# A two-layer decoder trunk on one core: projections and NSA scores as single plain float32 matmuls on unsplit operands

## The chip, the core and the metric

The kernel runs on one core of a Trainium2 chip. The core has TensorE (matmuls, written PE in the profile, its weight loads PEld), VectorE (DVE), ScalarE (ACT), GpSimd (POOL) and SyncE (SP), which here issues all transfers between HBM and the on-chip memory. The metric is the device time of one execution in microseconds, as the median of several runs.

## What is computed

Two layers, each on 256 tokens of width 1024: a modulation of the condition vector, a normalised and modulated input h, one projection to 3864 columns, two attention groups on them (MoBA, which here is plain causal attention, and NSA with a compressed, a selected and a window branch), a gated concatenation y, an output projection, a norm and a gated residual. Cut to what matters here:

```python
def reference(x, c, w_ada, ..., w_in, w_out, ...):
    cs = jax.nn.silu(c)
    for l in range(DEPTH):                        # 2
        mod = cs @ w_ada[l] + b_ada[l]
        shift, scale, gate = ...
        h = rmsnorm(x, g_pre[l]) * (1.0 + scale) + shift
        u = h @ w_in[l]                           # 256 x 1024 @ 1024 x 3864
        (qm, km, vm, zm, qn, kc, vc, ks, vs, kw, vw, gl, zn) = split(u)
        # per head: softmax(q k^T - slope * distance) v; NSA: three branches, gated by sigmoid(gl)
        y = concat([o_m * silu(zm), o_n * silu(zn)])
        y = y @ w_out[l]                          # 256 x 1024 @ 1024 x 1024
        x = x + gate * rmsnorm(y, g_post[l])
    return x
```

All inputs and the output are float32.

## The kernel before

Every projection is a sum over 8 row blocks of 128. Its operands are split into a high part, rounded to float32r, and a low part, the rest: `split_hi` and `split_lo` (lines 360 to 374) make `hi` and `lo` of each weight unit of 128 x 1024 on ScalarE or VectorE, and h and y are kept as `hH`, `hL` and `yH`, `yL`. `mm3` (lines 396 to 401) then makes one product from three float32r matmuls: low by high, high by low, high by high. Most have 256 moving columns; the token projection of the first stage (line 839) has 512, the combined one of layer 1 and the rest of the values 280. The scores of NSA's two full branches (lines 586, 587) are two float32r matmuls, of a query tile that holds the high part on one half of the partitions and the low part on the other (`qs`), with the keys' low and high parts (`kL`, `kH`). MoBA's scores (615, 617), all products of probabilities and values (596 to 630), the modulation (216) and the matmuls that only keep the array busy (283) are plain float32. Transposes (565 and others) are matmuls with the identity in a mode of their own.

The first layer's start (`first_layer_start`, from line 774) is in the order in which it is written: five stages of 1, 1, 2, 2 and 2 row blocks, each with the next stage's modulation between its column blocks. All that follows is put in order by the framework's scheduler from the steps in `PLAN`, so that projections of one step fill TensorE between the attention steps of another. A letter d in a step sends the high parts to VectorE. Weights come in units of up to 512 KB through the pool `raw` (8 buffers), and go from there to the pool `split` (8 buffers each of `hi` and `lo`). SyncE issues their loads in order, each as soon as its buffer is free. `out_mm` is the output projection of one token tile, `post` the norm and residual behind it, `hnorm` the next layer's h. `tables` writes the distance biases (`bias`, `cbias`) before the first attention.

## Time and profile before

| | us |
|---|---|
| median of 3 runs | 356.67 (354.29 to 356.84) |
| profiled execution, first to last instruction | 354.4 |
| PE busy | 341.4 |
| DVE busy | 266.1 |
| ACT busy | 204.3 |
| mean DMA rate | 201 GB/s |

The profiled execution's time is known as its span, 354.4 us; the runs without a profile lie between 0.1 us below and 2.4 us above it. A busy time sums the lengths of instructions. A matmul's length in the profile is its way through the array, some 280 ns for most, while the next one starts earlier; what a matmul costs in a stream is the distance from its start to the next start. A plain float32 matmul that is no transpose stands in the trace as two MATMUL records, each with a weight load: line 283 has 20 matmuls in the program and 40 records.

### The profile page before, as it was taken

To read this page: it belongs to the slowest core of one execution; us is meant where nothing else is said; L and a number is where in the kernel's file an instruction comes from. 1 tells how busy PE (TensorE), PEld (TensorE's weight loads), DVE (VectorE), ACT (ScalarE), POOL (GpSimd) and SP (SyncE) were. 2 spreads that over 40 slices of the span, in tenths; PEclk is the share of its full clock that TensorE was granted. 3 is DMA by queue.
4 is the path that set the end of the run, shared out by engine and by line. 5 is a ranking of instruction groups with operands and counts; after the bars stand their busy time and mean duration, and the time that the engine had idled before them with its cause. 6 is when DMAs were issued, how large, how long until landed. Compare 5 with 4: busy or idle time off the path is not lost.

```text
span 354.4 us, 7595 instructions
## 1 busy us (share of the span) xinstructions
PE 341.4 (96%) x2852; PEld 299.6 (85%) x2852; DVE 266.1 (75%) x727; ACT 204.3 (58%) x506; POOL 10.5 (3%) x23
## 2 busy tenths in 40 slices
PE   7999999999999999989999999999999999999993
PEld 7789889988887878767998999998878898677993
DVE  2648669999987898879898985999987646776132
ACT  4423407776989863757365455543889655668211
POOL 2000001100000000000011000000000000000000
PEclk9999999999999999999999999999999999999998
DMA  7999999939955566899755798489454330000111
GB/s 237 321 331 353 350 338 220 308 108 354 347 186 154 167 217 210 259 351 333 197 149 162 223 284 247 130 285 352 130 160 139 119 120 2 0 2 1 62 60 59
DMA packets 72060, 71.12 MB, mean 201 GB/s; under 512 B 11440, under 2 KB 61784, under 8 KB 72024
## 3 DMA queue, kind: packets, MB, share of 16 engines
q1 hardware_dynamic: 72024, 70.65, 64.1%
q8 instruction: 22, 0.36, 0.4%
q14 instruction: 14, 0.11, 0.1%
HBM read 69.58 MB, written 1.06 MB: 199 GB/s over the span
## 4 chain that ended last, share of the span: by engine, by line
PE 73%; DVE 13%; DMA 6%; issue 4%; ACT 2%; POOL 1%; SPq 1%; DVEq 0%; POOLq 0%; ACTq 0%
PE pj L399 13%; PE pj L400 13%; PE pj L401 13%; PE tr L565 5%; DVE lo L372 4%; PE av L602 3%; PE tr L216 3%; DMA yL<-in_w_ada_dram 2%; DMA raw<-in_w_out_dram 2%; PE av L627 2%; PE sc L586 2%; PE sc L617 2%; PE av L604 2%; PE pj L839 2%; PE av L596 2%
## 5 line engine op out<-in xcount | busy, mean ns | idle before, releaser
L372 DVE TENSOR_TENSOR lo<-raw,hi 128x1024 fp32r<-128x1024 f32 (+3 forms) x82 | 90.7, 1123 | 15.9 <-ACT hi L364 15.5
L399 PE MATMUL pj<-hH,lo 128*128 128x256 f32 x320 | 93.1, 291 | 0.0
L400 PE MATMUL pj<-hL,hi 128*128 128x256 f32 x320 | 92.5, 289 | 0.0
L401 PE MATMUL pj<-hH,hi 128*128 128x256 f32 x320 | 92.1, 288 | 0.0
L364 ACT CAST hi<-raw 128x1024 fp32r<-128x1024 f32 (+4 forms) x70 | 66.0, 966 | 22.7 <-PE pj L401 17.1
L399 PEld LDWEIGHTS pj<-hH,lo 128*128 128x128 f32 x320 | 61.0, 191 | 4.4 <-issue 3.4
L400 PEld LDWEIGHTS pj<-hL,hi 128*128 128x128 f32 x320 | 61.0, 191 | 2.2 <-issue 1.7
L401 PEld LDWEIGHTS pj<-hH,hi 128*128 128x128 f32 x320 | 61.0, 191 | 1.4 <-issue 1.1
L548 ACT ACTIVATE S<-S,mn 128x128 f32<-128x128 f32 (+1 forms) x96 | 42.7, 448 | 4.4 <-DVE mn L545 4.1
L233 DVE SCALAR_TENSOR_TENSOR acc<-raw,cs,acc 128x512 f32<-128x512 f32 x49 | 36.5, 747 | 1.6 <-DMA raw<-in_w_ada_dram 1.2
L545 DVE CUSTOM_DVE_ANT_0 S<-sc,bias 128x128 f32<-128x128 f32 (+1 forms) x96 | 31.6, 350 | 7.6 <-PE tr L565 3.1
L399 PE MATMUL pj<-hi,yL 128*128 128x256 f32 x112 | 31.9, 285 | 0.0
L401 PE MATMUL pj<-hi,yH 128*128 128x256 f32 x112 | 31.9, 286 | 0.0
L400 PE MATMUL pj<-lo,yH 128*128 128x256 f32 x112 | 31.8, 285 | 0.0
L565 PE MATMUL tr<-ident,S 128*128 128x128 f32 x144 | 29.6, 281 | 0.0
L570 ACT COPY PT<-tr 128x384 f32<-128x384 f32 x44 | 20.3, 478 | 10.0 <-PE tr L565 9.9
L565 PEld LDWEIGHTS tr<-ident,S 128*128 128x128 f32 x144 | 17.5, 140 | 6.7 <-issue 3.0
L555 ACT ACTIVATE S<-S,sm 128x256 f32<-128x256 f32 (+1 forms) x46 | 20.4, 483 | 2.9 <-DVE sm L550 1.4
L399 PEld LDWEIGHTS pj<-hi,yL 128*128 128x128 f32 x112 | 21.2, 189 | 0.9 <-issue 0.9
L401 PEld LDWEIGHTS pj<-hi,yH 128*128 128x128 f32 x112 | 21.1, 189 | 0.5 <-issue 0.5
L400 PEld LDWEIGHTS pj<-lo,yH 128*128 128x128 f32 x112 | 21.0, 188 | 0.3 <-issue 0.3
L548 ACT ACTIVATION_READ_ACCUMULATOR S<-S,mn 128x1 f32 x96 | 18.3, 190 | 0.0
(248 smaller groups left out, 650.1 us busy)
## 6 DMA issues: line engine op xcount, KB each, us to landing
raw<-in_w_in_dram SPq DMA_DIRECT2D x43, 512.0 KB, 4.5
raw<-in_w_ada_dram SPq DMA_DIRECT2D x32, 512.0 KB, 4.6
raw<-in_w_out_dram SPq DMA_DIRECT2D x16, 512.0 KB, 7.2
raw<-in_w_in_dram SPq DMA_DIRECT2D x9, 256.0 KB, 3.9
qs<-in_w_ada_dram SPq DMA_DIRECT2D x4, 512.0 KB, 7.2
yH<-in_w_ada_dram SPq DMA_DIRECT2D x4, 512.0 KB, 7.2
yL<-in_w_ada_dram SPq DMA_DIRECT2D x4, 512.0 KB
raw<-in_w_in_dram SPq DMA_DIRECT2D x9, 128.0 KB, 5.7
```

Source lines behind the costliest of these rows:

```text
L216: self.nc.tensor.matmul(pm[32 * r:32 * r + 32, :P], self.csz[:, k, :], raw[:, j, c * P:(c + 1) * P], start=first <= k < first + turns, sto ...
L233: nc.vector.scalar_tensor_tensor(out=out, in0=raw[:, j], scalar=self.cs[:, k:k + 1], in1=out, op0=OP.mult, op1=OP.add)
L364: self.nc.scalar.copy(hi[:, :nk * n], raw[:, :nk * n])
L372: self.nc.vector.tensor_sub(lo[:, :nk * n], raw[:, :nk * n], hi[:, :nk * n].bitcast(F32))
L399: nc.tensor.matmul(out, aL, bH, start=first, stop=False)
L400: nc.tensor.matmul(out, aH, bL, start=False, stop=False)
L401: nc.tensor.matmul(out, aH, bH, start=False, stop=last)
L545: nc.vector.tensor_tensor_reduce(out=s[:, a:b], in0=sc[:, a:b], in1=self.bias[:, h, S - (b - a):S], scale=-1.0, scalar=3.0e38, op0=OP.add, ...
L548: nc.scalar.activation(s[:, a:b], s[:, a:b], AF.Exp, bias=mn[:, i:i + 1], scale=-1.0, accum_out=sm[:, i:i + 1])
L555: nc.scalar.activation(s[:, a:b], s[:, a:b], AF.Copy, scale=sm[:, i:i + 1])
L565: nc.tensor.transpose(pt[:, i * P:(i + 1) * P], blk, self.ident)
L570: nc.scalar.copy(ps, pt[:, :3 * P])
```

## The change

h, y, the weights, and NSA's queries and keys are kept once, as float32. Each product that `mm3` made of three float32r matmuls is now one plain float32 matmul; the score of NSA's full branches is one plain float32 matmul on the 64 partitions of the head, with the keys `ks` copied to both halves. All splitting is gone: the casts, the subtractions, the pool `split`, and the tiles of the second parts. The pool `raw` has 24 buffers, from which TensorE now reads the weights directly; the first layer's modulation weights, which had the place of later tiles, come through it too. The output weights come in units of 2 row blocks by 512 columns instead of 4 by 256, so that most of `out_mm` has 512 moving columns. The step letters d, now without meaning, are gone. Comments were removed, so all lines have other numbers. The core of the diff:

```diff
-0post0 1h0 0out1 0post1 1V00:d 1h1 1V10 0na 1A0 1V01:d 1C:d 1V11 1A1 1K:d 1Q0 1Q1 1cmp0
+0post0 1h0 0out1 0post1 1V00 1h1 1V10 0na 1A0 1V01 1C 1V11 1A1 1K 1Q0 1Q1 1cmp0
...
-            nc.scalar.copy(self.hH[:, ks, ts], hT[:, ks])
-            nc.vector.tensor_sub(self.hL[:, ks, ts], hT[:, ks], self.hH[:, ks, ts].bitcast(F32))
...
-        return raw, nk, n
-    def split_hi(self, unit, tags=None, eng=None):
-        raw, nk, n = unit
-        hi = self.tl(self.mp if tags else self.hp, [P, UNIT], tags[0] if tags else "hi", F32R)
-        if eng == 1 or eng is None and "d" not in self.how:
-            self.nc.scalar.copy(hi[:, :nk * n], raw[:, :nk * n])
-        else:
-            self.nc.vector.tensor_copy(hi[:, :nk * n], raw[:, :nk * n])
-        return hi
-    def split_lo(self, unit, hi, tags=None):
-        raw, nk, n = unit
-        lo = self.tl(self.mp if tags else self.hp, [P, UNIT], tags[1] if tags else "lo", F32R)
-        self.nc.vector.tensor_sub(lo[:, :nk * n], raw[:, :nk * n], hi[:, :nk * n].bitcast(F32))
-        return (hi[:, :nk * n].rearrange("p (k c) -> p k c", k=nk),
-                lo[:, :nk * n].rearrange("p (k c) -> p k c", k=nk))
-    def split(self, unit, tags=None):
-        """The two f32r parts of a unit (in slots of self.mp if tags are given)."""
-        return self.split_lo(unit, self.split_hi(unit, tags), tags)
-    def load_split(self, pieces, nk, n, tags=None):
-        return self.split(self.load(pieces, nk, n), tags)
-    def weights(self, w, cols, tags=()):
-        """Both f32r parts of the columns, a list over the 8 row blocks."""
+        return rv
...
-            hv, lv = self.load_split([wv[:, k0:k0 + nk, a:b] for a, b in cols], nk, n,
-                                     tags[k0 // step] if k0 // step < len(tags) else None)
-            parts += [(hv[:, j], lv[:, j]) for j in range(nk)]
+            v = self.load([wv[:, k0:k0 + nk, a:b] for a, b in cols], nk, n)
+            parts += [v[:, j] for j in range(nk)]
...
-    def mm3(self, out, aH, aL, bH, bL, first, last):
-        """out (+)= a.T @ b from f32r parts: low terms first."""
-        nc = self.nc
-        nc.tensor.matmul(out, aL, bH, start=first, stop=False)
-        nc.tensor.matmul(out, aH, bL, start=False, stop=False)
-        nc.tensor.matmul(out, aH, bH, start=False, stop=last)
...
-            hv, lv = parts[k]
-            self.mm3(pj[:, :n], self.hH[:, k, ts], self.hL[:, k, ts], hv, lv, k == 0, k == KK - 1)
+            self.nc.tensor.matmul(pj[:, :n], self.h[:, k, ts], parts[k],
+                                  start=k == 0, stop=k == KK - 1)
...
-                self.mm3(pj[:, b * S + lo:b * S + hi], hv[:, bs], lv[:, bs],
-                         self.hH[:, k, lo:hi], self.hL[:, k, lo:hi], k == 0, k == KK - 1)
+                self.nc.tensor.matmul(pj[:, b * S + lo:b * S + hi], parts[k][:, bs],
+                                      self.h[:, k, lo:hi], start=k == 0, stop=k == KK - 1)
...
-                q = self.qs[j][:, b, qt * P:(qt + 1) * P]
-                nc.tensor.matmul(o, q, self.kL[:, g, :, :nk], start=True, stop=False)
-                nc.tensor.matmul(o, q, self.kH[:, g, :, :nk], start=False, stop=True)
+                rows = slice(j * HD, (j + 1) * HD)
+                nc.tensor.matmul(o, self.qn[rows, b, qt * P:(qt + 1) * P],
+                                 self.ks[rows, g, :, :nk], start=True, stop=True)
...
-        y = self.tl(self.mp, [P, S], "ytmp", bufs=1)
-        nc.vector.scalar_tensor_tensor(out=y, in0=av[:, :S], scalar=0.5,
+        nc.vector.scalar_tensor_tensor(out=self.y[:, blk, :], in0=av[:, :S], scalar=0.5,
                                        in1=self.z[blk // 4][:, blk % 4, :],
                                        op0=OP.mult, op1=OP.mult)
-        nc.scalar.copy(self.yH[:, blk, :], y)
-        nc.vector.tensor_sub(self.yL[:, blk, :], y, self.yH[:, blk, :].bitcast(F32))
...
-        for c in range(4):
-            hv, lv = self.load_split([w[:, k0:k0 + 4, c * 256:c * 256 + 256]], 4, 256)
-            for j in range(4):
-                self.parts[c, k0 + j] = (hv[:, j], lv[:, j])
+        for c in range(2):
+            for k in range(k0, k0 + 4, 2):
+                v = self.load([w[:, k:k + 2, c * 512:c * 512 + 512]], 2, 512)
+                for j in range(2):
+                    self.parts[c, k + j] = v[:, j]
...
-            for c in range(a // 256, b // 256):
-                for k in k4:
-                    hv, lv = self.parts[c, k]
-                    self.mm3(pos[i][:, c * 256 - a:c * 256 - a + 256], self.yH[:, k, ts],
-                             self.yL[:, k, ts], hv, lv, k == 4 and c * 256 == a,
-                             k == 3 and c * 256 + 256 == b)
+            for k in k4:
+                v = self.parts[a // 512, k][:, a % 512:a % 512 + b - a]
+                self.nc.tensor.matmul(pos[i][:, :b - a], self.y[:, k, ts], v,
+                                      start=k == 4, stop=k == 3)
...
-        self.kH = self.tl(self.tp, [P, NG, 2, S], "wide", F32R)
-        self.kL = self.tl(self.tp, [P, NG, 2, S], "wide", F32R)
+        nc = self.nc
+        self.ks = self.tl(self.mp, [P, NG, 2, S], "ks")
         v = pj.rearrange("p (i k) -> p i k", i=2)
         half = [slice(0, HD), slice(HD, P)]
         for g in range(NG):
-            for r in (g, 1 - g):
+            for r in range(2):
                 if r == g:
-                    nc.scalar.copy(self.kH[half[r], g], v[half[g]])
+                    nc.scalar.copy(self.ks[half[r], g], v[half[g]])
                 else:
-                    nc.vector.tensor_copy(self.kH[half[r], g], v[half[g]])
-        for g in range(NG):
-            for r in range(2):
-                nc.vector.tensor_sub(self.kL[half[r], g], v[half[g]],
-                                     self.kH[half[g], g].bitcast(F32))
+                    nc.vector.tensor_copy(self.ks[half[r], g], v[half[g]])
...
-            for n, (h, v) in enumerate(((self.hH, w[0]), (self.hL, w[0]), (self.hH, w[1]))):
-                for t in range(NT):
-                    for j, k in enumerate(ks):
-                        nc.tensor.matmul(pA[t], h[:, k, t * P:(t + 1) * P], v[:, j],
-                                         start=(k == 0 and n == 0), stop=(k == KK - 1 and n == 2))
+            for t in range(NT):
+                for j, k in enumerate(ks):
+                    nc.tensor.matmul(pA[t], self.h[:, k, t * P:(t + 1) * P], w[:, j],
+                                     start=k == 0, stop=k == KK - 1)
...
-                self.mm3(dst[:, (b % 2) * S:(b % 2 + 1) * S], w[0][:, j, bs],
-                         w[1][:, j, bs], self.hH[:, k], self.hL[:, k],
-                         k == 0 and b % 2 == 0, k == KK - 1 and b % 2 == 1)
+                nc.tensor.matmul(dst[:, (b % 2) * S:(b % 2 + 1) * S], w[:, j, bs], self.h[:, k],
+                                 start=k == 0 and b % 2 == 0, stop=k == KK - 1 and b % 2 == 1)
...
-            hT = self.tl(self.wp, [P, n, S], "S")
             for j, k in enumerate(ks):
-                nc.vector.tensor_scalar(hT[:, j], xT[k // 4][:, k % 4], self.mod[:, 8 + k:9 + k],
-                                        self.mod[:, k:k + 1], op0=OP.mult, op1=OP.add)
-            hi = self.split_hi(uw[0], None, HIGH_ENGINE[s])
-            nc.scalar.copy(self.hH[:, kc], hT)
-            nc.vector.tensor_sub(self.hL[:, kc], hT, self.hH[:, kc].bitcast(F32))
-            w = [self.split_lo(uw[0], hi)] + [self.split(u) for u in uw[1:]]
+                nc.vector.tensor_scalar(self.h[:, k], xT[k // 4][:, k % 4],
+                                        self.mod[:, 8 + k:9 + k], self.mod[:, k:k + 1],
+                                        op0=OP.mult, op1=OP.add)
+            w = uw
...
-            self.rp = self.pool("raw", bufs=8)
-            self.hp = self.pool("split", bufs=8)
+            self.rp = self.pool("raw", bufs=24)
```

At the first stage of the start, TensorE's rows before (`av` from line 283 is the matmul that only keeps the array busy; `pj` and `sc` are sums in PSUM, `tr` transposes; the operands stand as moving, stationary):

```order
L283 MATMUL av_213<-ident 128x128 x6
L839 MATMUL pj_220<-hi_228,hH_167 128x512
L839 MATMUL pj_221<-hi_228,hH_167 128x512
L839 MATMUL pj_220<-hi_228,hL_168 128x512
L839 MATMUL pj_221<-hi_228,hL_168 128x512
L839 MATMUL pj_220<-lo_232,hH_167 128x512
L839 MATMUL pj_221<-lo_232,hH_167 128x512
L813 MATMUL tr_267<-ident,z_149 128x128 x4
L813 MATMUL tr_273<-ident,modG_153 128x128 x4
L399 MATMUL pj_222<-hH_167,lo_236 128x256
L400 MATMUL pj_222<-hL_168,hi_234 128x256
L401 MATMUL pj_222<-hH_167,hi_234 128x256
```

and now:

```order
L277 MATMUL av_209<-ident 128x128 x6
L764 MATMUL pj_216<-raw_109,h_164 128x512
L764 MATMUL pj_217<-raw_109,h_164 128x512
L739 MATMUL tr_240<-ident,z_146 128x128 x4
L739 MATMUL tr_246<-ident,qn_150 128x128 x4
L772 MATMUL pj_218<-h_164,raw_113 128x256
```

Six matmuls became two, and three became one, in the same places; the operands come straight from `raw` and `h`.

At the first scores of NSA's full branches in layer 0, TensorE's rows before (`wide` is kL or kH, `qs` the query of both parts):

```order
L586 MATMUL sc_1151<-wide_883,qs_135_909 128x256
L587 MATMUL sc_1151<-wide_882,qs_135_909 128x256
L400 MATMUL pj_1354<-hL_168,hi_1344 128x256
L401 MATMUL pj_1354<-hH_167,hi_1344 128x256
L399 MATMUL pj_1354<-hH_167,lo_1352 128x256
L400 MATMUL pj_1354<-hL_168,hi_1350 128x256
```

and now:

```order
L544 MATMUL sc_764<-ks_595,qn_616 128x256
L544 MATMUL sc_777<-ks_595,qn_616 128x512
L544 MATMUL sc_802<-ks_595,qn_616 128x256
L554 MATMUL av_763<-pct_734,vx_707 64x256 x2
L381 MATMUL pj_945<-h_164,raw_941 128x256 x2
L544 MATMUL sc_815<-ks_595,qn_616 128x512
L523 MATMUL tr_790<-ident,S_766 128x128
L523 MATMUL tr_796<-ident,S_766 128x128
```

A score is one matmul instead of two, and the projections between scores are single matmuls, one or two at a time.

On VectorE at the start of the program, the rows before (`cs` is silu(c), `rstd` the norm's factor):

```order
L137 MEMSET hmask 128x8
L145 MEMSET kbd 128x64
L165 SCALAR_TENSOR_TENSOR cs<-cth,tr_125 128x8
L167 TENSOR_SCALAR cs<-cs 128x8
L168 COPY csz<-cs 128x8
L303 SCALAR_TENSOR_TENSOR rstd_157<-ssq_150 128x1
L322 TENSOR_SCALAR z_149<-x_97,rstd_157 128x512 x2
```

and now:

```order
L134 MEMSET hmask 128x8
L142 MEMSET kbd 128x64
L110 TENSOR_SCALAR bias<-S_547 128x256 x8
L121 TENSOR_SCALAR cbias<-S_561 128x2x16 x8
L162 SCALAR_TENSOR_TENSOR cs<-cth,tr_122 128x8
L164 TENSOR_SCALAR cs<-cs 128x8
L165 COPY csz<-cs 128x8
L297 SCALAR_TENSOR_TENSOR rstd_154<-ssq_147 128x1
```

The tables, which used to follow the last stage's h, now stand ahead of silu(c): the buffer of their distances (`S`) is no longer taken by the unsplit h of the stages. On GpSimd their two distances and their masks moved ahead of the first `rstd` in the same way.

## Rows read from the trace of the kernel before

**Rows 1.** The page, parts 1, 2 and 4: busy time, granted clock, DMA in slices, chain.

```profile
PE 341.4 (96%) x2852; PEld 299.6 (85%) x2852; DVE 266.1 (75%) x727; ACT 204.3 (58%) x506; POOL 10.5 (3%) x23
...
PEclk9999999999999999999999999999999999999998
DMA  7999999939955566899755798489454330000111
...
PE 73%; DVE 13%; DMA 6%; issue 4%; ACT 2%; POOL 1%; SPq 1%; DVEq 0%; POOLq 0%; ACTq 0%
```

**Rows 2.** Busy time in two stretches, microseconds, instructions behind each.

```profile
55.00:75.00 20.00, 19.76 (x198) 18.70 (x196) 19.64 (x42) 14.92 (x29) 2.75 (x3) 1.00 0.74 202
200.00:220.00 20.00, 20.00 (x166) 19.83 (x165) 14.48 (x21) 9.40 (x17) 0.00 (x0) 1.00 0.89 244
```

**Rows 3.** Who TensorE waited for: total, times, longest, in microseconds.

```profile
PE tr L252 <- ACT accr L245: 2.0, 3, 1.2
...
PE tr L336 <- DVE wide L322: 1.2, 2, 0.7
PE pj L400 <- DVE lo L372: 0.9, 1, 0.9
```

**Rows 4.** The page, part 5: groups of instructions, busy time and mean ns.

```profile
L372 DVE TENSOR_TENSOR lo<-raw,hi 128x1024 fp32r<-128x1024 f32 (+3 forms) x82 | 90.7, 1123 | 15.9 <-ACT hi L364 15.5
L399 PE MATMUL pj<-hH,lo 128*128 128x256 f32 x320 | 93.1, 291 | 0.0
...
L364 ACT CAST hi<-raw 128x1024 fp32r<-128x1024 f32 (+4 forms) x70 | 66.0, 966 | 22.7 <-PE pj L401 17.1
```

**Rows 5.** TensorE in order of time: start, length, 59 to 66 us.

```profile
58.97 0.28 PE L399 MATMUL pj<-hH,lo 128*128 128x256 f32 x1
59.08 0.28 PE L400 MATMUL pj<-hL,hi 128*128 128x256 f32 x1
...
66.04 0.28 PE L401 MATMUL tr<-hH,hi 128*128 128x256 f32 x1
```

**Rows 6.** TensorE in order of time at 11.7 us, plain float32, two records a matmul.

```profile
11.74 1.50 PE L283 MATMUL av<-ident 128*128 128x128 f32 x12
```

**Rows 7.** Line 283: durations in ns, minimum, median, maximum.

```profile
L283 PE MATMUL av<-ident x40: 275/276/582, 1.4 to 13.0; 128*128 128x128 f32 x40
```

**Rows 8.** TensorE in order of time at 142 us: a float32 score, then float32r.

```profile
141.81 0.59 PE L617 MATMUL sc<-km,qm 64*128 64x256 f32 x2
142.33 0.39 PE L399 MATMUL pj<-hH,lo 128*128 128x256 f32 x1
142.55 0.28 PE L400 MATMUL pj<-hL,hi 128*128 128x256 f32 x1
```

**Rows 9.** Line 617: durations in ns, minimum, median, maximum.

```profile
L617 PE MATMUL sc<-km,qm x32: 376/377/480, 139.6 to 322.5; 64*128 64x256 f32 x32
```

**Rows 10.** TensorE in order of time at 100 us: transposes, NSA scores, projections.

```profile
100.31 0.27 PE L565 MATMUL tr<-ident,S 128*128 128x128 f32 x1
100.34 0.36 PE L401 MATMUL pj<-hH,hi 128*128 128x256 f32 x1
...
100.89 0.39 PE L587 MATMUL sc<-wide,qs 128*128 128x512 f32 x1
101.12 0.28 PE L399 MATMUL pj<-hH,lo 128*128 128x256 f32 x1
...
101.47 0.28 PE L399 MATMUL pj<-hH,lo 128*128 128x256 f32 x1
101.68 0.44 PE L602 MATMUL av<-PT,vsw 128*64 128x256 f32 x2
```

**Rows 11.** VectorE in order of time at 6 and at 54 to 62 us.

```profile
6.04 0.16 DVE L303 SCALAR_TENSOR_TENSOR rstd<-ssq 128x1 f32<-128x1 f32 x1 [2.57 <-ACT z L309]
...
54.60 0.89 DVE L113 TENSOR_SCALAR bias<-S 128x256 bf16<-128x256 f32 x4
...
60.83 1.71 DVE L124 TENSOR_SCALAR cbias<-S 128x32 f32<-128x32 f32 x8
```

**Rows 12.** GpSimd in order of time, 55 to 65 us.

```profile
60.98 1.10 POOL L114 TENSOR_SCALAR_AFFINE_SELECT bias<-bias 128x1024 bf16<-128x1024 bf16 x1 [18.16 <-DVE bias L113]
62.60 1.65 POOL L126 TENSOR_SCALAR_AFFINE_SELECT cbias<-cbias 128x128 f32<-128x128 f32 x2 [0.53 <-DVE cbias L124]
```

More of the change, by code (lines that the diff above doesn't have):

```diff
@@ L10 @@
 F32 = mybir.dt.float32
-F32R = mybir.dt.float32r
 BF16 = mybir.dt.bfloat16
@@ L784, in loads @@
             k, n = STAGES[s]
-            slots = []
-            while len(slots) < 2 * n:
-                tag, m = tags.pop(0)
-                t = self.tl(self.mp, [P, m, UNIT], tag)
-                slots += [t[:, i] for i in range(m)]
-            ada = self.ada_loads(l, spec[s], slots)
+            ada = self.ada_loads(l, spec[s])
             ks = slice(k, k + n)
```

53 lines of the change are left out of this document (14 added, 39 removed).

## The prediction

> **What bounds the kernel now.** I read the busy times first. TensorE (PE) is busy 341.4 of 354.4 us, VectorE 266.1, ScalarE 204.3; TensorE's granted clock stands at its upper level (2.4 GHz) in every slice but the last, and the chain that ended last is 73% TensorE [rows 1]. Busy TensorE time can hide slack, since lengths overlap, so the next look was at stretches. At 200 to 220 us nothing but TensorE is full. At 55 to 75 us VectorE is just as full (19.64 of 20), so the chain's 13% of VectorE could mean that the splits set the pace there [rows 2]. The order of time says no: from 58.97 to 66.04 us 60 float32r matmuls start at even distances, 7.07 / 59 = 0.120 us, with no hole [rows 5]. And the list of TensorE's waits is short, its three largest after the start being 2.0, 1.2 and 0.9 us in total [rows 3]. TensorE streams nearly all the time, VectorE and ScalarE run beside it. So the time after the change is, in the first place, the old time plus what TensorE gains or loses in issue.
>
> **What one product costs before and after.** Starts are what counts here, not lengths. Before: three float32r matmuls of 256 columns at 0.120 us, 0.360 us [rows 5]; with 512 columns one takes 101.12 - 100.89 = 0.23 us [rows 10]; with 280 about 0.130, on the line between.
>
> After: a plain float32 matmul. None with 128 rows, 128 stationary columns and 256 moving columns is in the trace, but two neighbours are. The array-warming matmul has the full array and 128 moving columns: 12 records last 1.50 us, the last of them 0.276, so a start every (1.50 - 0.276) / 11 = 0.111 us [rows 6, 7]. MoBA's score has 64 rows and 256 columns: two records last 0.59 us, the last 0.376, so 0.59 - 0.376 = 0.214 us between starts [rows 8, 9]. Twice the columns, twice the distance: a record costs about 0.0008 us a column and next to nothing besides, thus 0.216 for 256, 0.236 for 280, 0.431 for 512. The length grows with the columns too, 276 to 376 ns, as that of a float32r matmul does. Every plain float32 matmul is two records, so 0.432, 0.472 and 0.862 us. A float32r matmul goes past 256 columns in 0.120 us, a pair of plain records takes 3.6 times that. Three matmuls for one is no gain at this exchange.
>
> **The sum, part by part.** (a) The projections. The program has 544 products of 256 columns, 32 of 280 and 16 of 512 (320 of the first stand in one row [rows 4], the others in smaller ones). Before: 544 x 0.360 + 32 x 0.390 + 16 x 0.69 = 195.8 + 12.5 + 11.0 = 219.3 us. After, with the output projection in wider pieces: 448 of 256, 32 of 280 and 64 of 512 columns, 448 x 0.432 + 32 x 0.472 + 64 x 0.862 = 193.5 + 15.1 + 55.2 = 263.8 us. **Plus 44.5 us**. All of it lies on TensorE, which has no hole to take it.
>
> (b) The NSA scores, 16 of 256 and 16 of 512 columns: two float32r matmuls each before, 16 x 0.24 + 16 x 0.46 = 11.2 us, one plain one after, 16 x 0.432 + 16 x 0.862 = 20.7 us. **Plus 9.5 us.** They now use 64 rows of the array, and two scores of the two halves could run beside each other where they stand next to each other; the order shows that at few places, so I take nothing off, and 3 us for the low end.
>
> (c) Changes of the array's shape. Between a matmul on the full array and one on part of it TensorE loses some 0.09 us: line 399 to line 602 takes 101.68 - 101.47 = 0.21 instead of 0.12 [rows 10], and line 617 to 399 takes 0.31 (the second record starts at 142.02, the next matmul at 142.33) instead of 0.21; then the second float32r matmul waits another 0.10, 142.55 - 142.33 = 0.22 [rows 8]. The rows of TensorE in their order have 151 such changes before and 184 after, because the scores left the full shape: 33 x 0.09 = +3.0 us. The second wait, 44 times before, should vanish in a record that lasts 0.21 anyhow: 44 x 0.10 = -4.4 us. Transposes end for free against a float32r matmul (100.34 - 100.31 = 0.03 us between starts [rows 10]); bursts of them that run into a projection or score fall from 79 to 54, each worth 0.08: +2.0 us. Together **plus 0.6 us**. What no row shows is whether a plain full-array matmul beside a transpose counts as a change of shape. If not, this stands; if so, 99 places pay 0.09 and the 54 ends cost 0.08 more, +13 us. I take the first, since float32r and transposes, also of different kinds, follow each other on the full array at no cost.
>
> (d) The splits. VectorE loses its 82 subtractions (90.7 us) and more, ScalarE the 70 casts (66.0 us) [rows 4]. This is beside TensorE's work and worth only the waits that it caused: 0.9 us for `lo`, part of the 1.2 before the transposes of layer 1's h [rows 3], and the steps between h's modulation and its first matmul. **Minus 2 us**; the bounds are 0 and 6, the whole of TensorE's waits behind the start. Chains around TensorE get shorter while TensorE gets slower, so I see no new wait on these two engines.
>
> (e) The transfers. The bytes stay, and DMA is near full only in slices up to some 55 us and a few later ones [rows 1]. TensorE now needs longer for each byte, and 24 buffers (up to 8 of them held by output weights) let loads run ahead. Cost 0; the cover is TensorE's own slowness, and without it the old waits for DMA, under 1 us each, would be back.
>
> (f) The tables at the start. On VectorE 2 x 0.89 + 1.71 = 3.5 us now stand ahead of silu(c) and the first `rstd`, where VectorE was idle for 2.57 us before 6.04 us and had 1.5 more before that [rows 11]; on GpSimd 1.10 + 1.65 = 2.75 us stand ahead of the first `rstd` power [rows 12]. If VectorE starts them at 1.5 us it is through at 5.0, GpSimd then at 6.7, and `rstd`, due at 6.2, is 0.5 late. The first modulation matmul waits for weights until 8.37, so 0 to 0.5 us; I take 0. The 3.5 us that VectorE saves at 54 to 62 us are worth nothing, as TensorE streams there.
>
> Sum: 44.5 + 9.5 + 0.6 - 2 = +52.6 us, from 354.4 to 407.0 us of span. The median of the runs is 2.3 us above that span; the forecast goes by it: 356.7 + 52.6 = **409 us**.
>
> **Rivals.** *Weight loads set the pace.* The float32r matmuls start every 0.120 us and each has a weight load; at 200 to 220 us the loads are busy 19.83 of 20 us [rows 2]. If the load, not the columns, made the 0.120, a plain record would take that too, and three loads would become two: 592 products x 0.120 saved is -71 us, also -2 for waits, thus 356.7 - 73 = **284 us**, much faster. It holds if records of 256 columns start less than 0.18 us apart. Against it: 0.214 with 256 columns and 0.111 with 128, each with one load [rows 6 to 9]. The Trainium skill, "Perfetto Trace Analysis", section "Identifying the Most-Contended Engine", says to judge TensorE's headroom by the busy share of its weight loads and not by that of matmuls; by that rule the 85% of PEld would make fewer loads a gain, as in this rival. The trace disagrees for plain float32, where the same one load goes with 0.111 or 0.214 us.
>
> *Transposes pay.* The 13 us of (c): **422 us**. For it: all plain matmuls of the trace that border on transposes, on parts of the array, pay. Against it: they also change the shape.
>
> *The second half's weights are not hidden.* If each of the 576 plain matmuls paid the 0.10 us of the second matmul after a change [rows 8], +58 us: **467 us**. Line 283 speaks against it, whose 40 records load weights each and keep 0.111 [rows 6, 7].
>
> *All waits go, and the scores run in pairs.* 409 - 4 - 3 = **402 us**, from the lower ends of (b) and (d).
>
> **How the numbers follow.** The forecast and the last rival, which is its lower edge, have 0.80; transposes that pay 0.12, hidden weights 0.03, weight loads that set the pace 0.04; 0.01 is left for anything near no change. The range runs from 354.3, the fastest run, + 52.6 - 7 = 400 to the 422 of the transposes, rounded to 399 and 424: it leaves out the third rival and the faster one. Slower by over 1%, which is about what a measurement here can tell from no change: 0.95; within 1%: 0.01; faster: 0.04.
>
> **What would show it.** Plain records of 256 columns 0.21 to 0.22 us apart in the start's last stage, which then takes 20 matmuls x 2 x 0.216 = 8.6 us for its ten column blocks instead of 7.2; TensorE the chain's main part, above 80%; VectorE near 145 us busy, ScalarE near 120; the last slices unchanged. Starts 0.12 apart would refute (a), 0.30 or more between the last record of a projection and a transpose would show (c) wrong, and long waits of TensorE for `raw` transfers would refute (e).

## The result, and the profile after

The changed kernel takes 414.88 us (median of 4 runs, 414.59 to 415.35) where the kernel before takes 356.26 (4 runs): a ratio of 1.166, 95% interval 1.162 to 1.169, so 16.6% slower. Its profiled execution took 414.95 us, with a span of 413.2; the span grew by 58.8 us. The forecast was 409 us in a range of 399 to 424. Direction and range held, and the time is 5.9 us above the forecast.

The page of the kernel after, parts 1, 2 and 4: busy time, granted clock and DMA in slices, chain by engine.

```profile
PE 402.5 (97%) x2164; PEld 280.4 (68%) x2164; DVE 159.2 (39%) x590; ACT 129.1 (31%) x401; POOL 8.2 (2%) x23
...
PEclk9999999999999999999999999999999999999998
DMA  8999999999673059986075369970000000000111
...
PE 94%; DVE 2%; ACT 1%; issue 1%; POOL 0%; POOLq 0%; DVEq 0%; ACTq 0%
```

Against [rows 1]: TensorE makes up 94% of the chain instead of 73%. VectorE is busy 159 us instead of 266 and ScalarE 129 instead of 204, and the kernel is slower: what left these engines had been holding next to nothing up. The granted clock stands at the upper level (2.4 GHz) in every slice but the last, as before, so no part of the loss is a slower clock. DMA all but stops in the last quarter, where TensorE still streams: the weights are there before TensorE wants them.

Who TensorE of the kernel after waited for (total, times, longest, in us); the three largest:

```profile
PE av L277 <- POOL ident masks.py:199: 1.7, 1, 1.7
PE tr L328 <- DVE wide L316: 1.2, 1, 1.2
PE tr L246 <- ACT accr L239: 0.8, 2, 0.4
```

No wait is for a weight transfer. The wait for `lo` [rows 3] is gone, and so is more than half of that for `accr`. What is left to explain lies in TensorE's own records. Its rows in order of time (start, length), in the last stage of the start and at 99 to 104 us:

```profile
64.34 1.89 PE L772 MATMUL pj<-h,raw 128*128 128x256 f32 x8
66.06 3.62 PE L772 MATMUL sc<-h,raw 128*128 128x256 f32 x16
69.52 1.89 PE L772 MATMUL av<-h,raw 128*128 128x256 f32 x8
71.24 1.89 PE L772 MATMUL tr<-h,raw 128*128 128x256 f32 x8
73.06 0.24 PE L395 MATMUL tr<-ident,pe 32*128 32x32 f32 x1
...
99.94 1.12 PE L544 MATMUL sc<-ks,qn 64*128 64x512 f32 x2
101.00 0.33 PE L523 MATMUL tr<-ident,S 128*128 128x128 f32 x1
...
102.45 0.70 PE L544 MATMUL sc<-ks,qn 64*128 64x256 f32 x2
103.08 0.70 PE L381 MATMUL pj<-h,raw 128*128 128x256 f32 x2
103.62 0.60 PE L523 MATMUL tr<-ident,S 128*128 128x128 f32 x4
```

The ten column blocks are 40 records from 64.34 to 73.06, 8.72 us, where the forecast said 8.6 and the float32r matmuls had taken 7.07 for 59 steps [rows 5]. A record of 256 columns is (66.06 - 64.34) / 8 = 0.215 us after the one ahead of it. At 99.94 something else is seen. The two records of one score of 512 columns take 1.06 us instead of 2 x 0.43, and at 102.45 the two of 256 columns take 0.63 instead of 0.43; the projection behind it takes 0.54. Each step on or off the 64-row shape costs some 0.2 us, also where it comes from another part of the array (ahead of 102.45 stands a matmul on 64 columns).

Added up over the whole trace from each record's start to the next, the projections' lines went from 236.3 to 276.9 us, the NSA scores from 12.9 to 24.6, and the whole row of TensorE from 346.8 to 405.3: 58.4 of the 58.8 us that the span grew. From the start of the last matmul to the end it is 6.1 us before and 6.2 after.

### The profile page after: what moved, and what is told of

The parts are those of the page before. It is cut to its first block, busy times and chain, and to the rows that moved or that the text cites. A ratio compares the mean times of both kernels' runs of the same rounds, so it can differ in the third digit from the quotient of the medians.

```text
span 413.2 us, 5878 instructions
## 1 busy us (share of the span) xinstructions
PE 402.5 (97%) x2164; PEld 280.4 (68%) x2164; DVE 159.2 (39%) x590; ACT 129.1 (31%) x401; POOL 8.2 (2%) x23
## 3 DMA queue, kind: packets, MB, share of 16 engines
HBM read 69.58 MB, written 1.06 MB: 171 GB/s over the span
## 4 chain that ended last, share of the span: by engine, by line
PE 94%; DVE 2%; ACT 1%; issue 1%; POOL 0%; POOLq 0%; DVEq 0%; ACTq 0%
PE pj L381 33%; PE pj L624 12%; PE sc L544 6%; PE pj L367 5%; PE tr L523 5%; PE sc L772 3%; PE pj L764 3%; PE av L560 3%; PE tr L210 2%; PE av L277 2%; PE av L585 2%; PE pj L772 2%; PE sc L624 2%; PE av L772 2%; PE tr L772 2%; PE av L562 1%
## 5 line engine op out<-in xcount | busy, mean ns | idle before, releaser
L381 PE MATMUL pj<-h,raw 128*128 128x256 f32 x608 | 146.0, 385 | 0.0
L381 PEld LDWEIGHTS pj<-h,raw 128*128 128x128 f32 x608 | 110.2, 190 | 21.9 <-issue 8.8
L624 PE MATMUL pj<-raw,y 128*128 128x512 f32 (+1 forms) x128 | 51.3, 544 | 0.0
L227 DVE SCALAR_TENSOR_TENSOR acc<-raw,cs,acc 128x512 f32<-128x512 f32 (+1 forms) x61 | 42.5, 697 | 2.6 <-DMA raw<-in_w_ada_dram 1.0
L624 PEld LDWEIGHTS pj<-raw,y 128*128 128x128 f32 x128 | 23.1, 190 | 19.1 <-issue 18.4
L367 PE MATMUL pj<-raw,h 128*128 128x256 f32 (+1 forms) x128 | 30.6, 392 | 0.0
L367 PEld LDWEIGHTS pj<-raw,h 128*128 128x128 f32 x128 | 23.8, 190 | 4.5 <-issue 0.4
L544 PE MATMUL sc<-ks,qn 64*128 64x256 f32 (+1 forms) x64 | 25.9, 518 | 0.0
L772 PE MATMUL sc<-h,raw 128*128 128x256 f32 x64 | 15.3, 384 | 0.0
L560 PE MATMUL av<-PT,vsw 128*64 128x256 f32 x64 | 15.2, 399 | 0.0
```

The costliest lines, as they stand in the source:

```text
L227: nc.vector.scalar_tensor_tensor(out=out, in0=raw[:, j], scalar=self.cs[:, k:k + 1], in1=out, op0=OP.mult, op1=OP.add)
L367: self.nc.tensor.matmul(pj[:, :n], self.h[:, k, ts], parts[k], start=k == 0, stop=k == KK - 1)
L381: self.nc.tensor.matmul(pj[:, b * S + lo:b * S + hi], parts[k][:, bs], self.h[:, k, lo:hi], start=k == 0, stop=k == KK - 1)
L544: nc.tensor.matmul(o, self.qn[rows, b, qt * P:(qt + 1) * P], self.ks[rows, g, :, :nk], start=True, stop=True)
L560: nc.tensor.matmul(o[:, :S], self.vsw[:, 0, vc], pts[j][i][:, :S], start=False, stop=False)
L624: self.nc.tensor.matmul(pos[i][:, :b - a], self.y[:, k, ts], v, start=k == 4, stop=k == 3)
```

## The experiments

Three theories stood at the beginning. **A**: each plain record costs TensorE 0.00084 us a moving column, its weight load is hidden, and only TensorE's row counts. **B**: the price is one for each record or each switch of kind, not one of columns. **C**: the split work on VectorE and ScalarE was itself holding the kernel before back. **D** and **P** in the expectations are named there each time. Runs 1 to 4, 5 to 8, and 9, 11 and 12 shared a chip and the runs of the kernel before; run 10 had its own.

**1. The output projection in 256 columns again** (kernel after; 32 more matmuls, of half the width):

```
-        for c in range(2):
-            for k in range(k0, k0 + 4, 2):
-                v = self.load([w[:, k:k + 2, c * 512:c * 512 + 512]], 2, 512)
+        for c in range(4):
+            v = self.load([w[:, k0:k0 + 4, c * 256:c * 256 + 256]], 4, 256)
```

> The changed kernel, with the output weights again in units of 4 row blocks by 256 columns, so that the output projection is 128 plain float32 matmuls of 256 columns instead of 48 of 512 and 32 of 256. Same columns, same bytes, 48 matmuls (96 records, 96 weight loads) more. Theory A (a plain record costs 0.00084 us a moving column, its weight load is hidden): 96 more matmuls x 2 x 0.216 less 48 x 2 x 0.429, +0.3 us, so 414 to 416 us. Theory B (each record pays something fixed of 0.1 us for its weights): 96 x 0.1 = +10 us, 424 us or more.

Measured: 417.0 us (416.6 to 417.05), ratio 1.172 (1.170 to 1.173), 2.1 us above the kernel after and 1 us above A's range, far from B's 424. Its trace has 96 more records on TensorE, 0.02 us each if the whole difference is theirs. The price lies in the columns and hardly in the records; B falls in the form of a price by the record.

**2. NSA scores on the whole array** (kernel after; the queries of each head in a tile of their own with zeros in the other half, so that the score is a plain 128-row matmul):

```
-                nc.tensor.matmul(o, self.qn[rows, b, qt * P:(qt + 1) * P],
-                                 self.ks[rows, g, :, :nk], start=True, stop=True)
+                nc.tensor.matmul(o, self.qz[j][:, b, qt * P:(qt + 1) * P],
+                                 self.ks[:, g, :, :nk], start=True, stop=True)
```

> The changed kernel, with NSA's scores on the full array: per head a query tile whose other 64 partitions are zero, against the keys on all 128. Still one plain float32 matmul a score, the same columns. The order then has 154 changes between the full array and a part of it instead of 174. Theory A with a price of 0.09 us for a change and 0.10 for the second record after it: 20 x 0.09 and some 30 x 0.10, -4 to -5 us, 410 us. If changes of shape cost nothing beyond noise: 414 to 416. If half-array scores gain by running beside each other: slower than 415.

Measured: 410.43 us (410.41 to 410.45), ratio 1.154 (1.152 to 1.155), 4.5 us below the kernel after. The matmuls have the same columns. The rows of TensorE have 172 changes of the array's shape instead of 202, so that the 4.5 us are 0.15 us for each of 30 changes that went (20 of them between the full array and a part of it, as the expectation counts). VectorE has 8 us more work, beside TensorE's.

**3. The scores alone** (kernel before, with plain 64-row scores on unsplit keys and queries; the projections keep their three matmuls):

```
-                nc.tensor.matmul(o, q, self.kL[:, g, :, :nk], start=True, stop=False)
-                nc.tensor.matmul(o, q, self.kH[:, g, :, :nk], start=False, stop=True)
+                nc.tensor.matmul(o, self.qn[rows, b, qt * P:(qt + 1) * P],
+                                 self.ks[rows, g, :, :nk], start=True, stop=True)
```

> The kernel before, with part (b) of the change alone: NSA's scores as one plain float32 matmul on 64 rows, keys and queries unsplit; projections still three float32r matmuls. Theory A: +9.5 us for the columns, and +2 to +4 for the shape changes (176 instead of 148, and second records that wait), 367 to 370 us. Theory C (the split work on VectorE and ScalarE is what TensorE waits for, so removing some gives time back): at or below 360.

Measured: 376.86 us (374.36 to 380.39), ratio 1.057 (1.052 to 1.062): about 20 us above the kernel before, more than A and far from C. The profiled execution has a span of 378.6 us at a mean granted clock of 0.986; the shortest of the four has one of 372.6 at 0.999. In the trace the scores' lines take 25.4 us instead of 12.9. The largest wait is new. Its row in the list of TensorE's waits:

```profile
PE sc L615 <- DVE mn L545: 3.4, 2, 3.3
```

The stretch behind it, busy times of PE, PEld, DVE, ACT and POOL, then the granted clock, DMA's share and GB/s:

```profile
150.00:165.00 15.00, 14.11 (x117) 10.24 (x117) 9.22 (x35) 8.86 (x28) 0.00 (x0) 0.68 0.50 168
```

And VectorE in order of time at the end of that wait:

```profile
149.80 0.49 DVE L231 TENSOR_SCALAR acc<-raw,cs 128x512 f32<-128x512 f32 x1 [2.96 <-DMA raw<-in_w_ada_dram]
150.21 0.28 DVE L545 CUSTOM_DVE_ANT_0 S<-sc,bias 128x128 f32<-128x128 f32 x1
```

VectorE stood 2.96 us at an ada sum (line 231) whose weights had not landed, with the softmax's first step (line 545) queued behind it. TensorE waited 3.3 us for that, and ran the stretch behind it at a mean clock of 0.68 of the upper level: 0.50, the lower of the two (1.2 GHz), from 150 to 158 us, then 2.4 GHz again. That is at most (1 - 0.68) x 15 = 4.8 us lost. So 12.5 + 3.3 + 4.8 of this execution's 24 us are named. The shortest execution, at a clock of 0.999, can't have lost so much in that way. For all four, the order that the scheduler made anew has 205 changes of shape instead of 167. At the 0.2 us that run 5 shows for one, 38 more are 7.6 us (a part of them stands in the scores' lines already). With the 9.4 us of the scores' columns this estimate gives 17 of the 18.8 us by which the shortest execution lies above the kernel before. What the others have on top is seen in the profiled one alone.

**4. One float32r matmul** (kernel before; the low parts of weights, h and y are left out of every projection, and not made):

```
-        nc.tensor.matmul(out, aL, bH, start=first, stop=False)
-        nc.tensor.matmul(out, aH, bL, start=False, stop=False)
-        nc.tensor.matmul(out, aH, bH, start=False, stop=last)
+        nc.tensor.matmul(out, aH, bH, start=first, stop=last)
```

> The kernel before with the low parts left out: one float32r matmul of the high parts a product instead of three, no subtractions for low parts of weights, h and y (so the projections are those of rounded operands). TensorE's issue falls by two thirds of 219 us, 146 us. Theory A: the time falls until transfers (70.65 MB, at 350 GB/s 202 us) and the attention's chains set the pace, 215 to 260 us. If TensorE's issue is not what sets the time: above 300 us.

Measured: 301.94 us (300.66 to 303.21), ratio 0.849 (0.844 to 0.853), above what A allowed, and just in the range (above 300) that the expectation gave to the case that TensorE's issue doesn't set the time. 54 us came off, so in the kernel before it set a good part of it; with 1184 fewer matmuls TensorE no longer sets the time alone. Three of TensorE's waits:

```profile
PE pj L396 <- ACT hi L363: 13.8, 8, 6.4
PE tr L240 <- DVE acc L233: 8.2, 2, 7.0
PE tr L216 <- DMA yL<-in_w_ada_dram: 4.2, 2, 3.8
```

The page's chain by engine:

```profile
PE 48%; ACT 19%; DMA 14%; DVE 10%; issue 4%; SPq 3%; POOL 0%; DVEq 0%; POOLq 0%; ACTq 0%
```

The casts on ScalarE, hidden before, are waited for, and the mean granted clock is 0.886. A's sum holds only as long as TensorE is the bound; here it is not.

**5. Mixes of matmuls, measured by themselves** (kernel after, with runs of matmuls at its end; one run, at a granted clock of 1.00):

```
+            for _ in range(12):
+                transposes()
+                plain(4)
...
+            for _ in range(12):
+                rounded(4)
+                half(4, True, 1)
...
+            half(16, True, 2)
+            plain(16)
+            half(16, False, 2)
```

> The kernel after, with runs of matmuls added at its end whose results nobody reads (so its time as a whole says nothing; their start-to-start times are read from the trace). Five mixes of twelve rounds each: four transposes and four plain 256-column matmuls; four transposes and four float32r ones; four plain 128-row and four plain 64-row ones; four float32r and four plain 64-row ones; four float32r and four plain 128-row ones. Then sixteen plain 64-row matmuls of 512 columns that alternate between the halves, and sixteen on one half. A (the prices belong to changes of array shape and kind, whatever the neighbours in the program): the fourth transpose lasts 0.10 to 0.11 us ahead of a plain matmul and 0.02 to 0.04 us ahead of a float32r one, and the second record after a change to the 64-row shape lasts 0.31 to 0.33 us instead of 0.216. P (the prediction's step): the fourth transpose lasts the same ahead of both, and the second record after a change lasts 0.216. For the alternation A expects 0.43 us a record on one half and 0.52 on two, P 0.43 on both.

TensorE in order of time, one round of each mix and the long runs (line 928 transposes, 932 plain, 936 float32r, 942 plain on 64 rows; a plain matmul is two records):

```profile
406.49 0.60 PE L928 MATMUL tr<-ident,h 128*128 128x128 f32 x4
406.92 1.89 PE L932 MATMUL pj<-h 128*128 128x256 f32 x8
408.65 0.60 PE L928 MATMUL tr<-ident,h 128*128 128x128 f32 x4
...
432.48 0.60 PE L928 MATMUL tr<-ident,h 128*128 128x128 f32 x4
432.83 0.72 PE L936 MATMUL pj<-wide 128*128 128x256 f32 x4
433.39 0.60 PE L928 MATMUL tr<-ident,h 128*128 128x128 f32 x4
...
446.32 1.99 PE L932 MATMUL pj<-h 128*128 128x256 f32 x8
448.25 1.14 PE L942 MATMUL sc<-h 64*128 64x256 f32 x8
449.31 0.48 PE L932 MATMUL pj<-h 128*128 128x256 f32 x1
...
480.93 0.74 PE L936 MATMUL pj<-wide 128*128 128x256 f32 x4
481.60 1.13 PE L942 MATMUL sc<-h 64*128 64x256 f32 x8
482.66 0.39 PE L936 MATMUL pj<-wide 128*128 128x256 f32 x1
...
507.18 1.89 PE L932 MATMUL pj<-h 128*128 128x256 f32 x8
508.72 0.83 PE L936 MATMUL pj<-wide 128*128 128x256 f32 x4
509.39 0.38 PE L932 MATMUL pj<-h 128*128 128x256 f32 x1
...
533.53 7.14 PE L942 MATMUL sc<-h 64*128 64x512 f32 x32
540.60 7.17 PE L932 MATMUL pj<-h 128*128 128x256 f32 x32
547.71 14.00 PE L942 MATMUL sc<-h 64*128 64x512 f32 x32
561.63 7.17 PE L932 MATMUL pj<-h 128*128 128x256 f32 x32
```

Four things are read off:

- *Transposes and kinds.* A round of four transposes and four plain matmuls lasts 408.65 - 406.49 = 2.16 us, and 4 x 0.109 + 8 x 0.216 = 2.16. With float32r it lasts 433.39 - 432.48 = 0.91, and 4 x 0.109 + 4 x 0.120 = 0.92. Neither pays for the neighbourhood. The last transpose is shorter ahead of float32r (432.83 - 432.48 = 0.35 for four instead of 0.43), as A said; but the first float32r matmul gives it back. Float32r and plain matmuls in turn (507.18 to 509.39, 2.21 us, against 4 x 0.120 + 8 x 0.216 = 2.21) cost nothing extra either.
- *Shape.* 32 plain records between two runs of 64 rows take 540.60 to 547.71, 7.11 us, where 32 x 0.216 is 6.91: half a change at each end, 0.2 us for a whole one. In the trace the last record ahead of a change takes 0.309 us instead of 0.216, and the first behind it 0.320: the second record waits, as A said and P not. With float32r in place of the plain matmuls a round lasts 1.73 us (480.93 to 482.66) instead of 2.99 (446.32 to 449.31). The difference, 1.26, is that of the records alone, 8 x 0.216 - 4 x 0.120 = 1.25. So a change of shape costs a plain matmul exactly what it costs a float32r one.
- *Halves side by side.* Sixteen plain matmuls of 512 columns on one half of the array last 547.71 to 561.63, 13.92 us. On the two halves in turn they last 533.53 to 540.60, 7.07: two neighbours run beside each other at the price of one.
- *Where both were wrong.* The alternation costs nothing, where A had expected 0.52 us a record and P 0.43. What looked like it at 99.94 us above (1.06 us for two records) is the change of shape.

The Trainium skill, "TensorEngine Tiling (Array Packing)", section "Key Properties", says that a change of the tiling mode, unlike one of the tile, drains TensorE, and that different tiles can run in parallel. The runs agree with both: 0.2 us for a change of shape and nothing for one of the half, and 7.07 instead of 13.92 us for sixteen matmuls on two halves.

**6. TensorE's work kept, the low parts not made** (kernel before; each projection is three float32r matmuls of its high parts, so its output is that product three times over):

```
-            nc.vector.tensor_sub(self.hL[:, ks, ts], hT[:, ks], self.hH[:, ks, ts].bitcast(F32))
...
-        self.nc.vector.tensor_sub(lo[:, :nk * n], raw[:, :nk * n], hi[:, :nk * n].bitcast(F32))
```

> The kernel before with three float32r matmuls of the high parts alone: every projection is its high parts' product, three times over, and no low part of weights, h or y is made. TensorE's work is the same, VectorE loses the subtractions (some 100 us of them). A (the split work lay beside TensorE): 350 to 356 us, so 0 to 1.5% faster than before. C (the split work held TensorE up, and its removal is worth something): 345 us or less.

Measured: 359.49 us (358.85 to 361.36), ratio 1.012 (1.008 to 1.016). VectorE fell from 266 to 175 us of busy time and the kernel became 4 us slower. C falls for VectorE's part; the casts on ScalarE (204 us busy, as before) are still made here, so that theirs is not tested. A expected a small gain, and there is none; the instructions stand in another order and have 173 changes of shape instead of 167, which is 1.2 us. The other 3 are not settled. They are a yardstick: an edit of the kernel before that adds no work to TensorE moved the time by 4 us.

**7. The output projection alone as plain float32** (kernel before; 128 matmuls of 256 columns on unsplit y and weights):

```
-                    self.mm3(pos[i][:, c * 256 - a:c * 256 - a + 256], self.yH[:, k, ts],
-                             self.yL[:, k, ts], hv, lv, k == 4 and c * 256 == a,
-                             k == 3 and c * 256 + 256 == b)
+                    self.nc.tensor.matmul(pos[i][:, c * 256 - a:c * 256 - a + 256],
+                                          self.y[:, k, ts], self.parts[c, k],
```

> The kernel before with the output projection alone as plain float32 matmuls of 256 columns on unsplit operands (128 matmuls; eight buffers of their own for its weights). A (a cost for each plain record): 128 times 0.07 us is 9 us, 363 to 368 us. B (a cost of going from one kind to the other, or one that comes only when TensorE has nothing else): under 361 us or over 371.

Measured: 372.1 us (370.61 to 373.48), ratio 1.046 (1.042 to 1.051), 16.5 us above the kernel before, beyond what A allowed and in the upper range of B. By start to start the new matmuls' line takes 57.8 us, 0.227 a record with its waits and changes, and the 384 float32r matmuls that went had taken 49.0: +8.8, where A had 9. A's term came, and B's cost of going from one kind to the other is refuted by the mixes of run 5. The other 8.0 us of the row are spread over many lines, none with more than 2.6 (4.3 in the float32r matmuls that stayed), and are twice the yardstick above; what made them is open.

**8. 12 weight buffers instead of 24** (kernel after):

```
-            self.rp = self.pool("raw", bufs=24)
+            self.rp = self.pool("raw", bufs=12)
```

> The kernel after with 12 weight buffers instead of 24. A (TensorE sets the pace and the transfers have room): within 1.5% of the kernel after, 413 to 421 us. D (the 24 buffers carry the weights over, and the prefetch is what keeps TensorE fed): 425 us or more.

Measured: 414.82 us (414.56 to 420.8), against 414.88 with 24. For this kernel 24 buffers are worth nothing over 12. That each weight is now read for longer would explain it; no run here shows it.

**9. Scores of two heads as neighbours** (kernel after; 20 weight buffers and five work buffers):

```
+            for j in range(2):
+                o = scs[j][:, :2 * nk].rearrange("p (i k) -> p i k", i=2)
+                rows = slice(j * HD, (j + 1) * HD)
+                nc.tensor.matmul(o, self.qn[rows, b, qt * P:(qt + 1) * P],
+                                 self.ks[rows, g, :, :nk], start=True, stop=True)
+            for j in range(2):
+                h = 2 * b + j
+                s[j].append(self.softmax(scs[j], h, [(0, nk), (nk, 2 * nk)],
```

> The kernel after with the NSA scores of a block's two heads one behind the other for each query tile, so that the plain 64-row matmuls on the two halves of the array are neighbours (five work buffers instead of three, and 20 weight buffers instead of 24, make room). By the added runs of matmuls two such neighbours take the time of one (0.432 us a pair at 256 columns, 0.858 at 512). A (TensorE's records and the changes of array shape are all that counts): eight pairs of 256 and eight of 512 columns are 10.3 us instead of 20.6, and some 16 changes of shape fewer at 0.2 us are 3 more: 399 to 403 us. D (the softmax behind the scores sets the pace of these blocks, since both score banks are now taken at once): within 1% of the kernel after, or slower.

Measured: 415.09 us (414.84 to 416.15), no gain. The scores' line did shrink, from 24.6 to 18.5 us by start to start, and the changes from 202 to 187. The trace shows where it went. In TensorE's list of waits:

```profile
PE tr L446 <- DVE gelu L441: 3.7, 1, 3.7
```

VectorE in order of time:

```profile
272.22 0.75 DVE L227 SCALAR_TENSOR_TENSOR acc<-raw,cs,acc 128x512 f32<-128x512 f32 x1 [1.92 <-DMA raw<-in_w_ada_dram]
273.01 0.16 DVE L432 COPY pbias<-sc 128x1 f32<-128x1 f32 x1
```

And the busy times of 270 to 280 us, in the columns of run 3:

```profile
270.00:280.00 10.00, 6.28 (x26) 3.88 (x25) 4.35 (x15) 0.60 (x2) 0.00 (x0) 0.74 0.98 333
```

VectorE's ada sums (line 227) waited for late weights, the compression's first step (line 432) stood behind them, and TensorE waited 3.7 us; the granted clock, 0.74 in the mean of these ten us, took up to 2.6 more. D's cause, the softmax, was not it.

**10. The same with 24 weight buffers** (and four work buffers instead of five; run 9 is the side with minus):

```
-            self.rp = self.pool("raw", bufs=20)
+            self.rp = self.pool("raw", bufs=24)
```

> The kernel of the run with paired scores, with 24 weight buffers again (and four work buffers). The run with 20 kept the scores' 6 us, but VectorE stood at 268 to 273 us behind transfers of ada weights that came late, and TensorE sat idle 3.7 us behind it, then ran at a lower clock. A (the buffers made those transfers late; TensorE's records and changes of shape set the time otherwise): 403 to 408 us. D (the paired order itself moves VectorE's work so that the hole stays): 412 us or more.

Measured: 408.6 us (408.34 to 408.72), ratio 1.149 (1.144 to 1.154): 6.3 us below the kernel after, 0.6 above A's range. The hole is gone (260 to 280 us are full), and the row of TensorE is 6.3 us shorter than that of the kernel after, with 6.6 less in the scores' line and 183 changes of shape instead of 202. The number of weight buffers was the suspect; the work buffers changed with it, so that the two are not told apart. TensorE in order of time:

```profile
92.42 0.70 PE L543 MATMUL sc<-ks,qn 64*128 64x256 f32 x4
93.05 0.65 PE L557 MATMUL av<-pct,vx 128*64 128x256 f32 x2
```

Two scores (four records) take 93.05 - 92.42 = 0.63 us here, where one took that at 102.45 in the kernel after. Less than the 10 us of the whole pairing came, since the scheduler put other work between many of the pairs: in 13 places of the 32 that full pairing would give, a record starts within 0.03 us of the one ahead of it.

**11 and 12. Weights rounded by the transfer**, without and with paired scores (kernel after; every projection one float32r matmul, the low parts left out, no cast on ScalarE or VectorE):

```
-        raw = self.tl(self.rp, [P, UNIT], "raw")
+        raw = self.tl(self.rp, [P, UNIT], "raw", F32R)
...
-            self.nc.sync.dma_start(rv[:, :, o:o + w], src)
+            self.nc.gpsimd.dma_start(rv[:, :, o:o + w], src)
```

> The kernel after with every projection as one float32r matmul: the weights are rounded to float32r by the transfers themselves, which GpSimd issues, and h and y are written as float32r, so that there is no cast or subtraction on ScalarE or VectorE. The low parts of weights, h and y are left out. A (TensorE's records set the time until another limit is met): projections of 219/3 = 73 us instead of 263 take 190 us away, which would be 225; the transfers (70.7 MB at the 350 GB/s of the busiest slices are 202 us) and the waits at the two ends keep it between 225 and 270. D (transfers that round and are issued by GpSimd are slower than those on SP's queue, or stand behind its other work): 300 us or more.

> The kernel of the run with rounding transfers, with the heads' scores paired as well. A: if TensorE still sets the time there, 8 to 14 us less than that run. D: if transfers or the softmax set it, within 3 us of that run.

Measured: 289.33 us (284.56 to 290.05; no interval) and 278.14 us (276.01 to 283.46), ratio 0.780 (0.776 to 0.784). The second is the fastest kernel of this study, 22% below the kernel before, but it computes the projections at the precision of one float32r product. The first lies above A's 225 to 270 and below D's 300. Two of the second's waits of TensorE:

```profile
PE tr L211 <- DMA raw<-in_w_ada_dram: 13.5, 7, 4.8
PE sc L428 <- DMA raw<-in_w_ck_dram: 11.0, 1, 11.0
```

Its DMA queues (packets, MB, share of 16 engines' span), the first of them GpSimd's:

```profile
q0 software_dynamic: 38528, 40.05, 63.2%
q1 hardware_dynamic: 29400, 30.60, 37.7%
```

TensorE waits 24.5 us for weights of two kinds, and the mean clock is 0.897. With the projections cheap, these transfers are what TensorE stands for next. The medians lie 11 us apart, but pairing is worth less: the one execution without it whose mean clock (0.890) is near that of the profiled one with it (0.897) took 284.56 us, against 277.54. That is 7 us, a little under A's 8 and clear of D's 3, from one execution.

## Why the prediction was right, and where it was mis-sized

**What bounds the kernel** was read rightly. VectorE at 75% and the chain's 13% of it were no bound: without its low parts it loses 91 us of work and nothing comes back (run 6). TensorE is 94% of the chain, where the prediction said above 80%. VectorE is busy 159 us and ScalarE 129, where it said 145 and 120; no wait hangs on that.

**(a) Projections, +44.5 us.** By the medians of the trace after, the projections' records are 896 of 256 columns (0.216 us), 64 of 280 (0.236) and 128 of 512 (0.429), together 263.6 us; before, by its medians, 1632 at 0.120, 96 at 0.129 and 48 at 0.228, together 219.2: +44.4. The price in columns, which came from neighbours with 128 columns and with 64 rows, held to a hundredth of a microsecond, and run 1 shows it to be one of columns. The Trainium skill, "FP8 and Floating Point Precision", section "TensorE Precision Notes", says that a true float32 product takes four passes; the trace is near it, with 2 x 0.216 / 0.120 = 3.6 times one float32r matmul.

**(b) NSA scores, +9.5 us.** By the same medians 32 records of 256 and 32 of 512 columns are 20.6 us, and before 32 float32r matmuls of 0.120 and 32 of 0.229 were 11.2: +9.4. Right, and the lower end, that they might run in pairs, was real but unused in the kernel after: none of its score records starts within 0.03 us of the one ahead. Run 10, with 13 such starts and 19 changes of shape fewer, gains 6.3 us by both together.

**(c) Changes of shape, +0.6 us: this is the step that failed.** It took three terms. *The count* was near: 33 more forecast, between the full array and a part of it; the trace has 28 more of these (154 and 182), and 35 more (167 and 202) with those between two parts, which pay as well. *The price of 0.09 us each* is half of what it is. The second wait of 0.10, which "should vanish in a record that lasts 0.21 anyhow", does not vanish; it comes on top of the record (540.60 to 547.71 in the mixes, and 0.63 instead of 0.43 at 102.45). So the -4.4 never came, and the +3.0 is 35 x 0.2 = 7.0 us, an estimate. *The transposes' ends, +2.0*, are no loss: what the last transpose saves ahead of float32r, the first float32r matmul pays. So (c) is +7.0 instead of +0.6, and these 6.4 us are the miss (5.9 us of the time, 6.2 of the span). Run 2 shows the price in the kernel itself, 4.5 us for 30 changes fewer; that is no more than the yardstick of run 6, so the mixes of run 5 are what settles it. The sign that the prediction named for a wrong (c), 0.30 us from a projection's last record to a transpose, did not come: it watched the transposes, and the failing term was the second record.

**(d) Splits, -2 us.** What (a) to (c) leave of the row's 58.4 us is 58.4 - 44.4 - 9.4 - 7.0 = -2.4. It agrees with TensorE's idle time, the span less the busy time of the two pages, which went from 13.0 to 10.7 us. The waits that the forecast named are seen to be shorter, by about 2 us; run 6 doesn't confirm a gain from the low parts, and how the rest is made up stays open.

**(e) Transfers, 0.** Right: no wait for a projection's weights, and half of the buffers give the same time (run 8). **(f) Tables, 0.** No wait of the start is longer than the identity's 1.7 us, which was 1.4 before, and the first modulation matmul starts at 8.70 us instead of 8.37, within the 0 to 0.5 that the prediction gave.

**The rivals.** Weight loads that set the pace (284 us): refuted by the 0.215 us distance in the trace, and the weight loads fell from 85 to 68% of the span while the time rose. Transposes that pay (422): refuted by the mixes. The second half's weights not hidden (467): refuted, since plain records in a row stay 0.216 us apart. Waits that all go, with scores in pairs (402): not the kernel after, but what run 10 goes towards.

**Luck.** That 414.9 us lies inside the range owes something to luck. The upper end was made for transposes that pay, and they don't; it had room for a price of shape changes that the prediction had at a tenth of its size.

## What to carry to other kernels

Price a change of number format by the columns that pass through the array, from any two rows of the same kind with different widths, before counting instructions: one plain float32 matmul for three float32r ones is three instructions for one, and 20% more of TensorE's time. Price every change of the array's shape by itself, and where a kernel must leave the full shape, do it for two halves at once, side by side. Work removed from an engine beside the bound bought next to nothing here; an engine beside the bound that stands at a late transfer, with a short step of a chain behind it, costs its wait and then the clock (runs 3 and 9).

## What the runs showed of the chip that was not expected

A change between the full array and 64 rows costs 0.2 us, for float32r and plain float32 alike: part before the change and part in the second record behind it. Two plain matmuls on the two halves take the time of one (7.07 us for sixteen of 512 columns in turn, 13.92 on one half). A transpose ahead of a float32r matmul ends early (four start to start in 0.35 us instead of 0.43), and the float32r matmul behind it starts its successor as much later. After waits of TensorE of 3.3 us (run 3) and 3.7 us (run 9) the granted clock stood at its lower level, 0.50, from 150 to 158 us and from 276 to 280 us.
